# First FFN of a hybrid decoder layer: early weight splits spread over the whole stage, gate and up in turns, and the column tiles of the mixing stage split there too

## The chip, the cores and the metric

The kernel runs on one core of a Trainium2 chip, in one launch. The metric is the device time in microseconds (us), from the median of several executions; a further execution is recorded by the hardware profiler.

## The reference

One layer of a decoder trunk on 1024 tokens of width 1024, with 16 learned meta tokens put in front. It computes, in float32:

```python
h = h + 0.5 * swiglu(rms_norm(h, ffn1_norm), ffn1_w_in, ffn1_w_out)
u = rms_norm(h, mix_norm) @ w_in
hq, hf, hi, hg, sq, sk, sv = split(u)            # 7 groups of 512 columns
o = concat([hgrn2(hq, hf, hi, hg), stick_breaking(sq, sk, sv)])
h = h + o @ w_out
h = h + 0.5 * swiglu(rms_norm(h, ffn2_norm), ffn2_w_in, ffn2_w_out)
```

`swiglu(x) = (silu(x @ W_gate) * (x @ W_up)) @ W_out` with 2816 hidden columns. `hgrn2` is a gated linear recurrence of 4 heads, and `stick_breaking` is a strictly causal attention of 8 heads whose weights are products of sigmoids. The meta tokens are dropped at the end.

## The kernel before, in words

**Precision.** TensorE multiplies in a float32 format of reduced precision. Each operand is therefore split into a high part (a cast on ScalarE, line 357 in the FFNs, 226 for other weights) and a low part (a subtraction on VectorE, lines 359 and 228), and each product is three matmuls: high by high, low by high, high by low. A weight tile comes raw from DRAM, and is split just before it is used.

**First FFN, input side** (`fast_in`). The 1040 positions lie in thirds of 352, 344 and 344 columns. Two thirds are computed together by a scheme of seven products in place of eight: a *quad* is a block of 256 hidden columns of gate or of up. Its seven products are named by the activation operands B11, T2, B21, T3, T1, T4 and B22, and accumulate in three PSUM banks: B11 and B21 in `qa`, T2, T3 and T4 in `qb`, T1 and B22 in `qc`. Between products VectorE copies a partial sum out of a bank (`kept`, line 458: u2 after T2, u3 after T3), and the next product in that bank waits for it. The weights of a quad are four raw blocks `a11, a21, a22, a12` and four sums of them, made by POOL (`made`, line 372). The remaining third (352 columns, *plain*) is multiplied with the raw blocks in the ordinary way, in bank `qd`. For the first three pairs of quads (the *openers*, about 75 to 165 us) the plain part runs ahead, and the pairs run afterwards, gate quad first, then up quad; from about 165 us the eight remaining pairs carry the plain products inside the quad (`also`), so that a quad has eleven products of twelve matmuls.

The order on TensorE is written out by hand (`manual_schedule`). On the other engines the framework's scheduler orders the instructions by its own model of time; `tc.issue_after(ins)` adds that what a block traces on the engine of `ins` is queued behind `ins`.

**Early splits.** `split_ahead` takes blocks of 128 by 512 weights through a small pipeline: load (groups of four blocks, one group ahead), for some blocks a sum on POOL (line 193), cast on ScalarE (168) and subtraction on VectorE (169) into a tile `both` (three buffers), store of both parts to DRAM (163). Each `next` of the generator advances it by one block. The kernel before does this for 28 blocks: the seven weight operands of four quads of the second FFN (`quad_group`), which later loads them split (`parted2`). The steps are advanced by `taken`, called after each eviction of the first FFN's main loop, once more than six quads are done: one step for each eviction until they are used up. `turn_x`, advanced by `between` after each quad, transposes x into a DRAM tensor.

**The middle.** `col_tile` and `split_w` (lines 209 to 229) load and split a weight tile of w_in (128 columns, 512 KB) or w_out (256 KB), or load its two parts where they lie in DRAM already (`self.parted`, empty in the kernel before). They are used by the attention's projections, by `hgrn_fill` (16 tiles of the recurrence: kinds v, f, q, g of four heads), which fills TensorE beside the attention, and by `mix_out`, which multiplies with w_out, half of it beside the recurrence. Two tiles (columns 2560 and 3072) are taken ahead, during step A22 of the first FFN's output side (`early_w`).

Of the kernel before, what the change touches and what calls it, by code (L numbers as in the profile page):

```python
# [20 lines left out]
P = 128  # L21
D = 1024
# [17 lines left out]
class Block:  # L40
# [141 lines left out]
    def quad_group(self, pool, w_in, col, dst):  # L182

        nc = self.nc
        views = [
            w_in[512 * h : 512 * h + 512, col + P * i : col + P * i + P]
            .rearrange("(k p) f -> p k f", p=P) for i, h in ((0, 0), (1, 0), (1, 1), (0, 1))
        ]
        s = {}

        def kept(name, op, x, y):
            t = s[name] = pool.tile([P, 512], F32, tag="sum", name="sum", bufs=3)
# [149 lines left out]
    def fast_in(self, ops, n, w_in, actD, openers, ev0, open_ev, feed=None, plain=None,  # L342
                between=lambda: None, after_opened=lambda: None, taken=lambda at: None):
# [44 lines left out]
        def weights(col, opened, also):  # L388
# [9 lines left out]
            s1 = made(a21, nc.gpsimd.tensor_add, a22)  # L398
            s2 = made(s1, nc.gpsimd.tensor_sub, a11)
            yield operand(s2)  # L400
            yield operand(a12)
            yield operand(made(a11, nc.gpsimd.tensor_sub, a21))
            yield operand(s1)
            yield operand(a22)
            yield operand(made(a12, nc.gpsimd.tensor_sub, s2))
            if also:
                yield operand(a21)
# [24 lines left out]
        def quad(col, take, opened=None, also=None):  # L432
            w = weights(col, opened, also)
# [13 lines left out]
            def first():  # L447
                p = go("a", "B11", True)
                p1 = ev0.tile([P, n], F32, tag="p1", name="p1", bufs=2 if plain else 2 * openers)
# [3 lines left out]
            def kept(name, x, y):  # L453
                if opened == "second":
                    t = wp.tile([P, n], F32, tag="s", name=name, bufs=3)
                else:
                    t = ev["p"].tile([P, n], F32, tag=name, name=name)
# [45 lines left out]
        def pair(f, opened=None, also=(None, None)):  # L503
# [32 lines left out]
            def combined():  # L536
# [20 lines left out]
                quad(f * P, gate, opened, also[0]),  # L557
                quad(D_FF + f * P, up, opened and "second", also[1]),
            ]

        ahead = range(0, 2 * openers, 2)
        if plain:
# [7 lines left out]
            for f in ahead:  # L570
                for q in pair(f):
                    drain(q)
                    between()
        else:
# [10 lines left out]
            for i in range(0, 2 * openers, 2):  # L585
                live = opened[i : i + 2]
                while live:
                    live = [q for q in live if next(q, live) is not live]
# [276 lines left out]

    def hgrn_fill(self, xh, xl, pool, dst):

        nc = self.nc
        plan = [(kind, h) for h in range(4) for kind in "vfqg"]
        first = {"v": 1024, "f": 512, "q": 0, "g": 1536}  # L870
# [23 lines left out]
        def weights(i):  # L894
            return self.col_tile(self.a["w_in"][0], first[plan[i][0]] + P * plan[i][1])
# [439 lines left out]
    def mix_out(self, k0, plan, o, ws, hD, hT, pool):  # L1335
# [4 lines left out]
        def part(m, half, k, kept):  # L1340
            c0, n = HALVES[half]
            if k == 0:
                if m not in ws:
                    ws[m] = self.split_w(
                        self.a["w_out"][0][k0 * P : (k0 + 4) * P, m * P : (m + 1) * P]
                        .rearrange("(k p) f -> p k f", p=P)
# [95 lines left out]
    def run(self):  # L1442
# [21 lines left out]
        with ExitStack() as c0:  # L1464
            with ExitStack() as c1:
                with tc.manual_schedule(engines={nc.tensor.engine}), ExitStack() as c2:
# [17 lines left out]
                    def ahead_of_time(pool):  # L1484

                        groups = []
                        for i in range(2):
# [9 lines left out]
                    def open_ev():  # L1497
# [4 lines left out]
                        turning.append(ahead_of_time(self.pool("ahead", ctx=c2)))  # L1502
                        return ev

                    def taken(at):
                        if len(seen) > 6:
                            with tc.issue_after(at.ins):
                                next(turning[1], None)

                    seen = []  # L1510

                    def between():
                        seen.append(len(seen))
# [29 lines left out]
                with tc.manual_schedule(engines={nc.tensor.engine}), ExitStack() as c2:  # L1543
# [62 lines left out]
                    def between(step, q):  # L1606
# [7 lines left out]
                        elif step == "A22":  # L1614
# [254 lines left out]
```

## Time and profile before

| | us |
|---|---|
| median of 3 runs | 2096.02 |
| lowest and highest | 2088.78, 2096.17 |
| the profiled execution | 2096.82 |
| its span in the trace | 2095.1 |

The stages in the profiled execution, by the trace: first FFN's input side to about 500 us, its output side to about 756, attention projections to about 925, attention with the recurrence's projections to about 1230, recurrence and output projection to about 1450, second FFN to the end. A row of the page or of a group names line, engine, operation, output tile and inputs, shape and count, then busy time and mean duration, then the idle time before the group and what ended it. A row of the timeline gives the start and the duration in us, and in brackets the idle time of the engine before it and what released it. PE is TensorE's matmul, PEld its weight load, DVE VectorE, ACT ScalarE, POOL GpSimd, SP the engine that issues most transfers.

### The profile page before, as it was taken

The page shows a single profiled execution, that of the slowest core. Times are in us where ns is not written, and L with a number is a line of the kernel's source. Part 1 is how long each engine was busy: PE and PEld are TensorE (multiplying, and loading weights), DVE is VectorE, ACT ScalarE, POOL GpSimd, SP SyncE. Part 2 cuts the span into 40 slices and gives each one's busy share as a digit, 9 for nine tenths or more (in the row PEclk, how much of TensorE's full clock was granted, in tenths as well). Part 3 has the DMA queues.
Part 4 walks back from the last instruction along what each step waited for, and adds up shares of the span by engine and source line. Part 5 has one row for each costly group of instructions (what it writes and reads, how often), then busy time and mean ns, then how long its engine had stood idle before and what let it go on. Part 6 is the DMA issues. An engine that isn't in the chain of part 4 may idle for free.

```text
span 2095.1 us, 32297 instructions
## 1 busy us (share of the span) xinstructions
PE 2028.8 (97%) x11520; PEld 1833.9 (88%) x11520; DVE 1397.9 (67%) x2140; ACT 899.7 (43%) x1860; POOL 646.5 (31%) x710
## 2 busy tenths in 40 slices
PE   7899999999999999999999999899999999999998
PEld 7899999999999989997888888778788888888887
DVE  6775874455479962338787857657567676676774
ACT  8543443323455643356666632334123233234443
POOL 2465664453000001234343310101155454440000
PEclk9999999999999999999999999999999999999999
DMA  7543874233866825443545162345633233359464
GB/s 193 172 154 123 276 253 144 89 96 119 296 208 211 258 82 176 135 172 97 145 126 141 62 231 74 96 121 176 210 117 111 93 108 101 106 197 328 137 196 136
DMA packets 280440, 328.39 MB, mean 157 GB/s; under 512 B 25911, under 2 KB 196279, under 8 KB 280279
## 3 DMA queue, kind: packets, MB, share of 16 engines
q1 hardware_dynamic: 262582, 275.88, 42.9%
q0 software_dynamic: 16656, 50.44, 6.5%
q8 instruction: 91, 1.49, 0.3%
q14 instruction: 71, 0.57, 0.1%
q10 hardware_dynamic: 1040, 0.00, 0.0%
HBM read 229.00 MB, written 97.25 MB: 156 GB/s over the span
## 4 chain that ended last, share of the span: by engine, by line
PE 77%; DVE 5%; issue 2%; ACT 1%; DMA 1%; POOL 1%; SPq 0%; DVEq 0%; POOLq 0%; ACTq 0%
PE o L697 16%; PE qb L413 11%; PE qa L413 8%; PE qc L413 7%; PE proj L243 5%; PE proj L244 5%; PE proj L245 5%; PE qd L413 4%; PE o L663 4%; PE flip L1177 2%; PE lvl L946 2%; PE wo L244 1%; PE wo L245 1%; PE wo L243 1%; DVE keep L1323 1%
## 5 line engine op out<-in xcount | busy, mean ns | idle before, releaser
L413 PE MATMUL qb<-T,wh 128*128 128x344 f32 (+1 forms) x1056 | 310.6, 357 | 9.1 <-DVE u L458 7.7
L359 DVE TENSOR_TENSOR wl<-s,wh 128x512 fp32r<-128x512 f32 x160 | 188.4, 1177 | 110.8 <-ACT wh L357 108.6
L413 PEld LDWEIGHTS qb<-T,wh 128*128 128x128 f32 x1056 | 193.2, 189 | 34.4 <-ACT wh L357 8.5
L697 PE MATMUL o<-parts 128*128 128x512 f32 x924 | 209.9, 389 | 0.0
L413 PE MATMUL qa<-B,wh 128*128 128x344 f32 (+1 forms) x696 | 206.2, 359 | 0.0
L243 PE MATMUL proj<-xh,wh 128*128 128x344 f32 (+2 forms) x576 | 204.9, 356 | 0.0
L697 PEld LDWEIGHTS o<-parts 128*128 128x128 f32 x924 | 173.3, 188 | 36.0
L244 PE MATMUL proj<-xh,wl 128*128 128x344 f32 (+2 forms) x576 | 199.4, 346 | 1.1 <-DVE wl L228 1.1
L245 PE MATMUL proj<-xl,wh 128*128 128x344 f32 (+2 forms) x576 | 198.7, 345 | 0.0
L413 PE MATMUL qb<-T,wl 128*128 128x344 f32 (+1 forms) x528 | 188.0, 356 | 0.0
L413 PE MATMUL qd<-X,wh 128*128 128x352 f32 x704 | 182.8, 327 | 1.6 <-DVE X L772 1.6
L359 DVE TENSOR_TENSOR wl<-raw,wh 128x512 fp32r<-128x512 f32 x160 | 148.5, 932 | 53.8 <-ACT wh L357 51.3
L357 ACT CAST wh<-s 128x512 fp32r<-128x512 f32 x160 | 99.4, 622 | 181.2 <-PE qb L413 130.0
L357 ACT CAST wh<-raw 128x512 fp32r<-128x512 f32 x160 | 98.6, 619 | 173.1 <-PE qc L413 88.5
L697 PE MATMUL o<-t,w 128*128 128x344 f32 x924 | 150.1, 323 | 3.8 <-DVE t L627 2.1
L697 PEld LDWEIGHTS o<-t,w 128*128 128x128 f32 x924 | 147.3, 189 | 5.5 <-DVE t L627 3.1
L413 PEld LDWEIGHTS qa<-B,wh 128*128 128x128 f32 x696 | 126.5, 188 | 15.5
L1323 DVE TENSOR_TENSOR_SCAN keep<-keep 128x144 f32<-128x144 f32 (+6 forms) x112 | 128.6, 1151 | 6.5 <-ACT keep L1319 4.4
L372 POOL TENSOR_TENSOR s<-raw 128x512 f32<-128x512 f32 x80 | 113.5, 1418 | 60.9 <-DVE wl L359 48.8
L1328 POOL TENSOR_TENSOR sig<-sig,keep 128x144 f32<-128x144 f32 (+3 forms) x64 | 87.0, 1360 | 138.8 <-DVE keep L1323 85.9
L413 PEld LDWEIGHTS qd<-X,wh 128*128 128x128 f32 x704 | 126.7, 192 | 1.8 <-DVE X L772 1.8
L413 PE MATMUL qa<-B,wl 128*128 128x344 f32 (+1 forms) x348 | 124.1, 357 | 0.7 <-DVE wl L359 0.7
(342 smaller groups left out, 4601.3 us busy)
## 6 DMA issues: line engine op xcount, KB each, us to landing
raw<-in_ffn_w_in_dram SPq DMA_DIRECT2D x184, 256.0 KB, 3.2
raw<-in_ffn_w_out_dram SPq DMA_DIRECT2D x176, 256.0 KB, 3.9
w2in<-both SPq DMA_DIRECT2D x28, 512.0 KB, 3.8
raw<-in_w_in_dram SPq DMA_DIRECT2D x28, 512.0 KB, 4.2
ks<-kD SPq DMA_DIRECT2D x32, 260.0 KB, 5.7
wh<-w2in SPq DMA_DIRECT2D x27, 256.0 KB, 3.1
wl<-w2in SPq DMA_DIRECT2D x27, 256.0 KB, 3.2
ak<-in_ffn_w_out_dram SPq DMA_DIRECT2D x22, 256.0 KB, 5.3
```

The lines of the kernel that those rows point to most:

```text
L243: nc.tensor.matmul(ps, wh[:, s], xs, start=k == 0, stop=False)
L244: nc.tensor.matmul(ps, wl[:, s], xs, start=False, stop=False)
L245: nc.tensor.matmul(ps, wh[:, s], xl[:, k, c0 : c0 + n], start=False, stop=k == nk - 1)
L357: nc.scalar.copy(hi, src)
L359: nc.vector.tensor_sub(lo, src, hi.bitcast(F32))
L372: op(t, x, y)
L413: nc.tensor.matmul(ps, a[:, k, :], b[:, k0 + k, :], start=start and k == 0 and i == 0, stop=k == 3 and i == 2, skip_group_check=True,)
L663: nc.tensor.matmul(ps[m], y[:, s], z, start=f == 0 and e == 0, stop=f == D_FF // P - 1 and e == 2,)
L697: nc.tensor.matmul(banks[bank][m], y[:, m * P : (m + 1) * P], z, start=start and q == 0 and e == 0, stop=q == nq - 1 and e == 2, skip_grou ...
L946: nc.tensor.matmul(ps[:, j, :], KB[:, META + c * P : META + (c + 1) * P], QA[:, c * P : (c + 1) * P], start=True, stop=True,)
L1323: nc.vector.tensor_tensor_scan(out=kv, data0=kv, data1=kv, initial=1.0 if last else keep[:, end : end + 1], op0=ALU.mult, op1=ALU.bypass,)
L1328: nc.gpsimd.tensor_mul(sig, sig, keep[:, 1 : nk + 1])
```

## The change

- The early splits are 78 blocks: 34 halves of 17 tiles of w_in (columns 2560, 3072 and 2048, and all of the recurrence's but the first two) and 16 tiles of w_out come first, then the 28 blocks of before.
- `taken` counts the evictions from the start. The first 36 advance nothing (12 of the plain openers, 24 of the opener pairs); from there 81 steps are spread over 88 evictions. POOL's sums of the first FFN are marked too, and each step is queued behind the latest marked instruction of every engine.
- The opener pairs run gate and up in turns, one product of each. Up's sums, its first partial sum and the partial sums u2, u3 get buffers of their own.
- In the main loop the second plain product with block a22 comes before T4 rather than after it.
- `quad_group` makes its last sum earlier, with two buffers for sums rather than three.
- The two tiles in step A22 are taken at its second and fourth rounds, rather than its sixth and eighth, and are not queued behind an eviction.

```diff
         return views, [
             ...
             (dst[2], lambda r: kept(2, sub, s[1], r[0])),
+            (dst[6], lambda r: kept(4, sub, r[3], s[2])),
             (dst[5], lambda r: r[2]),
             (dst[3], lambda r: kept(3, sub, r[0], r[1])),
-            (dst[6], lambda r: kept(4, sub, r[3], s[2])),
         ]
...
-        def made(x, op, y):
-            t = wp.tile([P, 4, P], F32, tag="s", name="s", bufs=3)
-            op(t, x, y)
+        def made(x, op, y, turns):
+            if turns == 2:
+                t = self.ahead.tile([P, 4, P], F32, tag="raw", name="s", bufs=8)
+            else:
+                t = wp.tile([P, 4, P], F32, tag="s", name="s", bufs=3)
+            taken(op(t, x, y), False)
             return t
...
+                if turns:
+                    yield
                 u2 = kept("u2", p1, go("b", "T2", True))
+                if turns:
+                    yield
                 take(0, 0, go("a", "B21", False), None)
+                if turns:
+                    yield
...
             take(1, 1, go("c", "T1", True), u3)
             yield
+            if also:
+                ready.append(next(w))
+                d = alone(None, ready[0], 1, True)
             take(1, 0, go("b", "T4", False), p1)
             yield
-            if also:
-                d = alone(None, last[0], 1, True)
             take(0, 1, go("c", "B22", False), u2)
...
+        def in_turns(live):
+            while live:
+                live = [q for q in live if next(q, live) is not live]
...
             for f in ahead:
-                for q in pair(f):
-                    drain(q)
-                    between()
+                in_turns(pair(f, None, (None, None), True))
+                between()
+                between()
...
+                        for col in [2560, 3072, 2048] + self.columns_of_heads()[2:]:
+                            t = self.parted[col] = self.dram.tile([P, 2, D], F32, name=f"win{col}")
+                            for h in range(2):
+                                pieces.append((
+                                    t[:, :, 512 * h : 512 * h + 512],
+                                    w_in[512 * h : 512 * h + 512, col : col + P]
+                                    .rearrange("(k p) f -> p k f", p=P),
+                                ))
+                        for k0 in (4, 0):
+                            for m in range(KT):
+                                ...
+                                self.parted[k0, m] = t
+                        groups += self.plain_groups(pieces)
...
-                    def taken(at):
-                        if len(seen) > 6:
-                            with tc.issue_after(at.ins):
+                    def taken(at, step=True):
+                        marks[at.ins.engine] = at.ins
+                        if not step:
+                            return
+                        seen.append(at)
+                        i = len(seen) - first
+                        if i > 0 and steps_ahead * i // hooks > steps_ahead * (i - 1) // hooks:
+                            with ExitStack() as c4:
+                                for ins in marks.values():
+                                    c4.enter_context(tc.issue_after(ins))
                                 next(turning[1], None)
+                    first, hooks, steps_ahead = 12 + 24, 88, 81
...
-                            if q in (5, 7):
-                                col = {5: 2560, 7: 3072}[q]
-                                with tc.issue_after(self.evicted.ins):
-                                    early_w.append(self.col_tile(a["w_in"][0], col))
+                            if q in (1, 3):
+                                early_w.append(
+                                    self.col_tile(a["w_in"][0], {1: 2560, 3: 3072}[q])
+                                )
```

More of the change, by code (lines that the diff above doesn't have):

```diff
@@ L386, in parted, with weights @@
             return got
-        def weights(col, opened, also):
+        def weights(col, opened, also, turns):
             if opened:
@@ L430, in plain_quad, with quad @@
                 take(i, ps)
-        def quad(col, take, opened=None, also=None):
-            w = weights(col, opened, also)
+        def quad(col, take, opened=None, also=None, turns=False):
+            w = weights(col, opened, also, turns)
             ps, ready, last = {}, [], []
@@ L448, in first @@
                 p = go("a", "B11", True)
-                p1 = ev0.tile([P, n], F32, tag="p1", name="p1", bufs=2 if plain else 2 * openers)
+                if turns == 2:
+                    p1 = ev["p"].tile([P, n], F32, tag="p1", name="p1")
+                else:
+                    p1 = ev0.tile(
+                        [P, n], F32, tag="p1", name="p1", bufs=2 if plain else 2 * openers
+                    )
                 self.last_p1 = nc.scalar.copy(p1, p)
@@ L501, in plain_pair, with pair @@
             return gate, up
[L503 removed]
+        def pair(f, opened=None, also=(None, None), turns=False):
             sg = {}
@@ L556, in pair @@
             return [
-                quad(f * P, gate, opened, also[0]),
-                quad(D_FF + f * P, up, opened and "second", also[1]),
-            ]
+                quad(f * P, gate, opened, also[0], turns and 1),
+                quad(D_FF + f * P, up, opened and "second", also[1], turns and 2),
+            ]
+        def in_turns(live):
+            while live:
+                live = [q for q in live if next(q, live) is not live]
         ahead = range(0, 2 * openers, 2)
@@ L585, in fast_in @@
             for i in range(0, 2 * openers, 2):
-                live = opened[i : i + 2]
-                while live:
-                    live = [q for q in live if next(q, live) is not live]
+                in_turns(opened[i : i + 2])
             after_opened()
```

38 lines of the change are left out of this document (25 added, 13 removed).

## The prediction

> **What bounds the kernel now.** I read the page first, then the stretches of the span (busy time of each engine, granted clock, DMA share), then, where TensorE lost time, the groups and the timeline. The page:
>
> ```profile
> PE 2028.8 (97%) x11520; PEld 1833.9 (88%) x11520; DVE 1397.9 (67%) x2140; ACT 899.7 (43%) x1860; POOL 646.5 (31%) x710
> ```
>
> TensorE (PE) is busy 97% of the span, so an edit that adds no matmul can only win back the time in which PE waits, or runs slowly. The next rows are stretches: length, busy time (and instructions) of PE, PEld, DVE, ACT and POOL, granted clock, DMA share and GB/s. The last three are narrow.
>
> ```profile
> 75.00:100.00 25.00, 20.41 (x109) 19.11 (x108) 11.54 (x18) 9.57 (x19) 12.24 (x10) 0.86 0.85 246
> 205.00:306.00 101.00, 96.28 (x600) 95.16 (x599) 83.06 (x101) 43.72 (x81) 65.62 (x64) 0.98 0.74 255
> 306.00:500.00 194.00, 194.00 (x1231) 193.43 (x1230) 98.79 (x145) 65.42 (x122) 94.88 (x102) 1.00 0.34 109
> 735.00:756.00 21.00, 17.71 (x104) 16.90 (x103) 18.69 (x41) 10.56 (x27) 0.00 (x0) 0.93 0.20 63
> 87.30:94.20 6.90, 6.45 (x20) 5.75 (x21) 4.71 (x6) 3.96 (x8) 6.18 (x5) 0.51 0.80 233
> 251.20:254.60 3.40, 3.40 (x14) 3.40 (x13) 3.37 (x5) 0.62 (x1) 2.71 (x3) 0.50 0.75 258
> 753.00:756.40 3.40, 3.40 (x14) 3.40 (x13) 1.07 (x3) 0.46 (x1) 0.20 (x1) 0.50 0.02 5
> ```
>
> From 306 to 500 us (first FFN, no early splits) PE never waits: 1231 matmuls in 194 us, 0.158 us each, so a product of twelve takes 1.9 us. A quad of the main loop is eleven products (seven, and four for the plain columns), 132 matmuls or 20.8 us; from 205 to 306 us, 600 matmuls, lie about 4.5 quads, and all but a few of the 28 early splits. The last three rows are spells at half clock, each behind a long PE wait; they cost about half their length: 3.3, 1.7 and 1.7 us.
>
> **Edit 1: splits bound behind the work before them, gate and up in turns (75 to 165 us).** The old early splits were ordered on one engine only, so some floated forward:
>
> ```profile
> 86.49 0.62 ACT L168 CAST both<-early 128x512 fp32r<-128x512 f32 x1 [7.32 <-DMA early<-in_ffn_w_in_dram]
> ...
> 87.68 0.66 PE L413 MATMUL qc<-T,wh 128*128 128x344 f32 x1 [3.82 <-ACT wh L357]
> ```
>
> ACT stood 7.32 us with an early cast at the head of its queue, until that cast's load landed; the cast that PE needed stood behind it, and PE waited 3.82 us. The new `marks` queue every step behind the latest marked instruction of ACT, DVE and POOL, and the first step comes after 36 evictions, behind all openers. So the wait and its half-clock spell go: 3.8 + 3.3 = 7.1 us. Two more openers lose time differently:
>
> ```profile
> L413 PE MATMUL qb<-T,wh 128*128 128x344 f32 x110 | 28.4, 322 | 3.0 <-DVE u L458 3.0
> ```
>
> T4 accumulates into the bank that DVE must first read as u3, and only T1 (1.9 us) lies between. In turns the up quad puts two products more there, 5.7 us in all: the 3.0 us go. What turns may add: up's first product comes second instead of eighth, so its four blocks are wanted earlier.
>
> ```profile
> 74.74 2.92 SPq L364 DMA_DIRECT2D raw<-in_ffn_w_in_dram  x5
> ```
>
> These five loads go out from 74.74 us, while the first quad's product starts at about 75. The cost lies between 0 (up's blocks are now requested before gate's sums, so they move forward in SP's queue) and 3.8 us (a wait as long as the one removed). The order of requests speaks for the low end: I take 1.5. Sum of edit 1: 7.1 + 3.0 − 1.5 = 8.6 us gained.
>
> **Edit 2: 78 blocks on 88 hooks, and the second plain product put ahead of T4 (165 to 500 us).** The dense stretch now loses this:
>
> ```profile
> L413 PE MATMUL qb<-T,wh 128*128 128x344 f32 x100 | 26.7, 331 | 4.7 <-DVE u L458 4.7
> ```
>
> The same wait of T4, 4.7 us in 4.5 quads, and behind the longest of them the spell at 251.2 us: 6.4 us together. The longest, with DVE's queue before it:
>
> ```profile
> 247.80 1.88 DVE L359 TENSOR_TENSOR wl<-raw,wh 128x512 fp32r<-128x512 f32 x1
> 249.61 0.50 DVE L458 TENSOR_TENSOR u<-qb,p 128x344 f32<-128x344 f32 x1
> ...
> 250.26 0.40 PE L413 MATMUL qb<-T,wh 128*128 128x344 f32 x1 [2.10 <-DVE u L458]
> ```
>
> The new order puts a plain product (1.9 us) between T1 and T4. It hides less than that, though: the plain product uses the same weights as T4, and their low half is the subtraction directly ahead of u3 in DVE's queue (ends 249.68, u3 ends 250.11). The wait moves to the plain product and is only 0.43 us shorter. So 4.7 − 4.5 × 0.43 = 2.8 us stay in 4.5 quads, 0.6 per quad.
>
> How long does such lag last now? Twelve hooks fall in two quads, so 88 hooks are 14.7 quads, and 81 steps are 5.5 a quad; the old rate was 28 in 4.5, 6.2. The bytes per time hardly change: 78 stores of 512 KB and 66 loads of 256 KB in 306 us are 190 GB/s, against 28 and 16 in 101 us, 187 GB/s, at a share of 0.74; more DMA waits are not due. VectorE's price:
>
> ```profile
> L359 DVE TENSOR_TENSOR wl<-raw,wh 128x512 fp32r<-128x512 f32 x18 | 19.6, 1090 | 1.5 <-ACT wh L357 1.5
> ...
> L169 DVE TENSOR_TENSOR both<-sum,both 128x512 fp32r<-128x512 f32 x16 | 18.6, 1163 | 3.0 <-ACT both L168 2.8
> L169 DVE TENSOR_TENSOR both<-early,both 128x512 fp32r<-128x512 f32 x12 | 12.6, 1048 | 3.3 <-ACT both L168 3.3
> ```
> ```profile
> L359 DVE TENSOR_TENSOR wl<-raw,wh 128x512 fp32r<-128x512 f32 x32 | 23.4, 733 | 32.9 <-ACT wh L357 31.5
> ```
>
> The same subtraction takes 1090 ns in the dense stretch and 733 after it. The 50 new blocks come first and need no POOL sums (the old 28 need 16), so their price lies between 0.73 and 1.16 us; I take 0.9, nearer the row without sums. DVE is then busy 51% (98.79 of 194) plus 5.0 of 20.8 us, some 75%, for 50 of 78 blocks (9.4 quads), and 82% as in the dense stretch for the last 28 (5.3 quads). Lag: 5.3 × 0.6 = 3.2 us, and 9.4 × 0.2 = 1.9 (0.2 is a choice between 0 at 51% and 0.6 at 82%). 6.4 − 5.1 = 1.3 us gained. Bounds: 6.4 gained if nothing waits, and the old price on all 14.7 quads (6.4 / 4.5 = 1.42 a quad, 20.9 us), 14.5 lost. Two-slot sums and the reordered T4 operand only bind POOL, which was busy 65% at most: nothing, or one sum late (1.3 us) at worst. ACT's 50 more casts of 0.62 us lift it from 34% to about 50%: hidden.
>
> **Edit 3: what leaves the middle.** At the end of the first FFN two column tiles were split in VectorE's busiest stretch (18.69 of 21 us); the first:
>
> ```profile
> 736.19 1.23 DVE L228 TENSOR_TENSOR wl<-raw,wh 128x1024 fp32r<-128x1024 f32 x1
> ...
> 747.86 2.00 PE L697 MATMUL o<-t,w 128*128 128x344 f32 x11 [1.58 <-DVE t L627]
> ...
> 751.58 0.42 PE L697 MATMUL o<-t,w 128*128 128x344 f32 x1 [1.71 <-DVE w L627]
> ```
>
> Twice 1.23 us leave a queue that is 3.3 us late, and the spell at 753 us (1.7) should go with the wait: 4.1, I take 4.0 (0 to 5.0). Four loads of 512 KB replace two on SP's queue, earlier, at a DMA share of 0.20. Further waits on splits:
>
> ```profile
> L244 PE MATMUL proj<-xh,wl 128*128 128x512 f32 x16 | 6.5, 404 | 1.1 <-DVE wl L228 1.1
> ```
> ```profile
> L244 PE MATMUL wo<-oH,wl 128*128 128x512 f32 x3 | 1.8, 584 | 1.5 <-DVE wl L228 1.5
> ```
>
> 2.6 us, near 781 and 1396 us. The split operands now come by DMA and need free buffers before they start; a raw tile of 512 KB took 4.2 us to land:
>
> ```profile
> raw<-in_w_in_dram SPq DMA_DIRECT2D x28, 512.0 KB, 4.2
> ```
>
> So each could also lose 2 us if its memory comes free as late as the old cast. I take 1.7 gained (−4 to 2.6). Between 925 and 1230 us the waits are these, and two of them follow a tile's split:
>
> ```profile
> L1177 PE MATMUL flip<-ident,sig 128*128 128x128 f32 x288 | 47.9, 275 | 11.2 <-DVE wu L1292 8.6 <-DVE wm L1292 2.5
> ```
> ```profile
> L228 DVE TENSOR_TENSOR wl<-raw,wh 128x1024 fp32r<-128x1024 f32 x14 | 20.8, 1485 | 10.1 <-ACT wh L226 10.0
> ```
> ```profile
> 1096.13 1.23 DVE L228 TENSOR_TENSOR wl<-raw,wh 128x1024 fp32r<-128x1024 f32 x1 [0.79 <-ACT wh L226]
> ...
> 1101.71 0.41 PE L1177 MATMUL flip<-ident,sig 128*128 128x128 f32 x2 [1.45 <-DVE wu L1292]
> ...
> 1163.72 1.23 DVE L228 TENSOR_TENSOR wl<-raw,wh 128x1024 fp32r<-128x1024 f32 x1 [0.19 <-ACT wh L226]
> ...
> 1168.66 0.52 PE L1177 MATMUL flip<-ident,sig 128*128 128x128 f32 x3 [1.83 <-DVE wu L1292]
> ```
>
> 20.8 us leave VectorE; I count the two waits, 3.2 us (0, if the scans alone make them, to 6, half of 11.2). The eight output tiles beside the recurrence I put at 0 (−2 to 2, the size of the two waits above): PE there follows a chain of short steps, not the splits.
>
> **Sum.** 8.6 + 1.3 + 4.0 + 1.7 + 3.2 = 18.8 us. The profiled execution took 2096.8 us (span 2095.1, 1.7 around it), 0.8 above the median: 2096.8 − 18.8 = **2078.0 us**.
>
> **Rivals.** *The old price on every hook*: each of 14.7 quads loses 1.42 us as now. For it: the wait's cause, the subtraction ahead of u3, stays. Against: 50 blocks without sums, and none of the quads near 180 us waits now. Edit 2 then loses 14.5: 2078.0 + 1.3 + 14.5 = 2093.8 us, no measurable change. *Slower: lag that drops the clock, quad after quad.* At 250.26 a wait of 2.10 us was followed by half clock: 2.1 + 1.7 = 3.8 us. If VectorE at 75 to 82% lags that far in every quad, the stage loses 14.7 × 3.8 = 55.9 instead of 6.4, so 2078.0 + 1.3 + 49.5 = 2128.8 us; it decides from about ten quads on (38 − 6.4 − 17.5, 14 slower). For it: the wait that shows it. Against: one spell in 4.5 quads, at a higher rate. The Trainium skill (TensorE: Matmul & The Clock Gate, HAM oscillation — how this bites in real kernels) warns of idle gaps above about 3.4 us only; by that rule a gap of 2.1 us keeps the clock and this rival would cost 2.1 × 14.7 = 30.9, 2103.8 us. The trace disagrees: 2.10 us sufficed. *The middle gives nothing*, since the loaded operands come as late as the old splits: 4.0 + 1.7 + 3.2 − 4.0 = 4.9 is lost of the sum (the emptied queue at 735 us stays): 2082.9 us.
>
> **How the numbers follow.** About 0.5%, 10.5 us, is what a measurement of this kernel can tell from no change. Chances: the forecast and its neighbours down to −10.5 us 0.53, the empty middle 0.11, the old price 0.23, the clock rival 0.13. Faster 0.64, same 0.23, slower 0.13. Low end: all good bounds, 10.1 + 6.4 + 5.0 + 2.6 + 6 + 2 = 32.1, 2065 us. High end: the old price with the turns' cost at 3.8, 2096 us. The clock rival is left out.
>
> **What would show it.** Right: no ACT wait on an early load and clock 1.00 from 85 to 95 us; no wait for u in the openers; early splits from about 170 to 475 us at an even rate; no L226 or L228 on the tiles of the recurrence; clock 1.00 from 735 to 760 us; flip's waits under 9 us. Wrong: PE waits above 1 us in most quads from 170 to 475 us with half-clock spells, PE waiting on a loaded wh or wl, or SP's queue standing before wh while other loads queue.

## The result and the profile after

| | before | after |
|---|---|---|
| median, us (5 runs each) | 2096.17 (2088.78 to 2098.8) | 2104.59 (2102.44 to 2108.25) |
| ratio of times | | 1.0042, 95% interval 1.0025 to 1.0058 |
| profiled execution, us | 2096.82 | 2104.59 |
| its span | 2095.1 | 2102.9 |

The change costs 8.4 us, 0.42%, where a gain of 18.8 us was forecast. That is less than the 10.5 us that the prediction named as the least a measurement can tell, but the interval lies clear of 1. The next table cuts the two spans at the first matmul of each stage, so that its rows sum to the spans.

| stage | before | after | gained | forecast |
|---|---|---|---|---|
| start (ahead of the openers' seven products) | 75.16 | 76.45 | −1.29 | 0 |
| openers | 95.86 | 94.96 | +0.90 | +8.6 |
| main loop of the first FFN | 345.63 | 360.79 | −15.16 | +1.3 |
| output side, first part | 84.88 | 84.88 | 0 | 0 |
| output side, second part, with step A22 | 155.60 | 155.97 | −0.37 | +4.0 |
| projections | 180.95 | 179.61 | +1.34 | +1.7 (both waits) |
| attention with the recurrence's projections | 303.96 | 299.63 | +4.33 | +3.2 |
| recurrence and output projection | 202.22 | 199.20 | +3.02 | (above) |
| second FFN | 650.86 | 651.35 | −0.49 | 0 |

The start lies between 74.7 and 78.4 us in the kernels run here, and its 1.3 us are within that. The page of after shows TensorE as well filled as before. The loss is many small waits, and 5.0 us more busy time for the same 11520 matmuls:

```profile
PE 2033.8 (97%) x11520; PEld 1836.0 (87%) x11520; DVE 1423.4 (68%) x2157; ACT 900.8 (43%) x1877; POOL 644.9 (31%) x710
```

The stretches of after, columns as in the prediction:

```profile
75.00:100.00 25.00, 19.40 (x103) 17.94 (x102) 12.67 (x17) 6.31 (x12) 11.34 (x11) 0.86 0.53 148
205.00:306.00 101.00, 96.67 (x607) 94.76 (x606) 73.95 (x100) 44.62 (x83) 46.41 (x51) 1.00 0.94 300
306.00:500.00 194.00, 185.36 (x1152) 182.08 (x1151) 150.01 (x178) 82.72 (x154) 119.55 (x118) 0.99 0.76 257
```

From 306 to 500 us PE was never idle before; now it does 1152 matmuls where it did 1231. The DMA share from 205 to 306 us is 0.94 against 0.74.

**Main loop.** First two groups of the stretch from 205 to 306 us of before, ScalarE's early casts, and then the same cast in the main loop of after (165 to 500 us), with the groups in which PE waits:

```profile
L168 ACT CAST both<-sum 128x512 fp32r<-128x512 f32 x15 | 9.2, 615 | 11.0 <-DMA w2in<-both 10.9
L168 ACT CAST both<-early 128x512 fp32r<-128x512 f32 x10 | 6.2, 615 | 6.3 <-DMA w2in<-both 6.3
```
```profile
L416 PE MATMUL qd<-X,wh 128*128 128x352 f32 x464 | 122.4, 327 | 3.4 <-ACT xts L849 3.4
L416 PE MATMUL qd<-X,wl 128*128 128x352 f32 x232 | 75.8, 327 | 7.1 <-DVE wl L359 7.1
L359 DVE TENSOR_TENSOR wl<-raw,wh 128x512 fp32r<-128x512 f32 x58 | 67.2, 1158 | 9.5 <-ACT wh L357 9.0 <-DMA raw<-in_ffn_w_in_dram 0.3
L168 ACT CAST both<-early 128x512 fp32r<-128x512 f32 x62 | 38.1, 615 | 65.5 <-DMA win<-both 27.3 <-DMA wout<-both 19.4 <-DVE both L169 6.0
```

A cast needs a free `both` tile, and a tile is free when its store to DRAM has landed. ScalarE stands 65.5 us with the cast at the head of its queue, 46.7 us of them for stores. The row was there before (10.9 and 6.3 us for w2in's stores), and I read past it. From 205 to 306 us alone, with 25 casts in both kernels, the stores account for 17.2 us before and 25.3 after. What stands behind the cast is late, here the copy of transposed x (L849):

```profile
256.38 0.62 ACT L168 CAST both<-early 128x512 fp32r<-128x512 f32 x1 [1.91 <-DMA win<-both]
...
260.50 0.57 ACT L849 COPY xts<-xt 128x512 f32<-128x512 f32 x1
...
261.12 0.43 PE L416 MATMUL qd<-X,wh 128*128 128x352 f32 x1 [0.80 <-ACT xts L849]
```

The transfers issued from 205 to 306 us, with count, size and median time to landing, before and then after:

```profile
w2in<-both SPq DMA_DIRECT2D x27, 512.0 KB, 3.7
early<-in_ffn_w_in_dram SPq DMA_DIRECT2D x7, 256.0 KB, 4.3
```
```profile
win<-both SPq DMA_DIRECT2D x25, 512.0 KB, 5.1
early<-in_w_in_dram SPq DMA_DIRECT2D x21, 256.0 KB, 5.3
early<-in_w_out_dram SPq DMA_DIRECT2D x5, 256.0 KB, 5.5
```

27 stores and 7 loads were 16.0 MB; 25 stores and 26 loads are 19.9 MB, 197 GB/s instead of 158.

**Openers.** SP's queue, PE's and POOL's in after, and a stretch of 11 us:

```profile
76.10 2.94 SPq L364 DMA_DIRECT2D raw<-in_ffn_w_in_dram  x5
```
```profile
87.00 0.66 PE L416 MATMUL qb<-T,wh 128*128 128x344 f32 x1 [2.43 <-ACT wh L357]
89.35 0.66 PE L416 MATMUL qb<-T,wl 128*128 128x344 f32 x1 [1.70 <-DVE wl L359]
```
```profile
67.71 5.13 POOL L375 TENSOR_TENSOR s<-raw 128x512 f32<-128x512 f32 x1 [5.25 <-DMA raw<-in_ffn_w_in_dram]
...
74.51 1.56 POOL L375 TENSOR_TENSOR s<-raw 128x512 f32<-128x512 f32 x1
83.24 1.28 POOL L375 TENSOR_TENSOR s<-raw 128x512 f32<-128x512 f32 x1 [7.17 <-DMA raw<-in_ffn_w_in_dram]
```
```profile
84.00:95.00 11.00, 6.88 (x29) 6.22 (x28) 5.15 (x6) 2.62 (x5) 5.87 (x7) 0.69 0.47 133
```

The cast held by an early load is gone, and so is every wait for u3 in this stage, but the blocks of the first pair land later than they are wanted. SP issues five loads at 76.10 us, when POOL's third sum has ended (74.51 + 1.56 = 76.07), and 0.35 us ahead of the pair's first product at 76.45. In the kernel before they left 0.42 us ahead (74.74 against 75.16), so the new order did not move them forward. POOL's first sum took 5.13 us here and 5.10 before, where the median of the kernel's 80 sums of two raw blocks is 1.30. POOL then waits 7.17 us for one of the loads, the sum is late, its cast and subtraction are late, and PE waits twice. A granted clock of 0.69 from 84 to 95 us shows a spell at half clock again, as behind the wait of before.

**Step A22.** The stage of after runs some 16 us later (its output side starts at 532.2 us, not 516.7), so the stretch that answers to 739 to 752 us there is about 723 to 736 us of before. SP's queue, the activation's landing and the stretch, before:

```profile
723.37 0.39 SPq L219 DMA_DIRECT2D raw<-in_w_in_dram  x1
724.85 0.32 SPq L617 DMA_DIRECT2D act<-act15T  x1
...
725.93 0.42 SPq L219 DMA_DIRECT2D raw<-in_w_in_dram  x1
```
```profile
act<-act15T SPq DMA_DIRECT2D x1, 172.0 KB, 3.5
```
```profile
720.00:741.00 21.00, 21.00 (x139) 21.00 (x138) 17.91 (x39) 15.97 (x35) 2.14 (x4) 1.00 0.84 260
```

And after, with the row of PE's wait:

```profile
739.98 0.38 SPq L214 DMA_DIRECT2D wh<-win  x1
...
741.36 0.43 SPq L214 DMA_DIRECT2D wl<-win  x1
...
743.15 0.67 SPq L634 DMA_DIRECT2D act<-act15T  x1
```
```profile
act<-act15T SPq DMA_DIRECT2D x1, 172.0 KB, 9.7
```
```profile
739.00:752.00 13.00, 13.00 (x85) 13.00 (x84) 10.16 (x21) 8.24 (x19) 2.13 (x4) 1.00 0.94 314
```
```profile
758.92 1.40 PE L279 MATMUL spread<-diag,ones_d 128*128 128x128 f32 x6 [3.17 <-DVE diag L276]
```

The engines were 84% busy there already. Nothing keeps the four loads of after apart (two lie between the rows shown), so SP sends 2 MB in a row where before sent 0.5 MB twice; the activation behind them takes 9.7 us to land instead of 3.5, and further on PE waits 3.17 us for the norm.

**The middle** did what was forecast. The attention's stretch, after:

```profile
L1199 PE MATMUL flip<-ident,sig 128*128 128x128 f32 x288 | 47.8, 275 | 7.5 <-DVE wu L1314 4.9 <-DVE wm L1314 2.5
L228 DVE TENSOR_TENSOR wl<-raw,wh 128x1024 fp32r<-128x1024 f32 x1 | 1.2, 1212 | 0.0
```

One split is left of 14, and flip waits 7.5 us instead of 11.2.

### The profile page after: what moved, and what is told of

It reads as the page before. It is cut to its first block, busy times and chain, and to the rows that moved or that the text cites. A ratio compares the mean times of both kernels' runs of the same rounds, so it can differ in the third digit from the quotient of the medians.

```text
span 2102.9 us, 32545 instructions
## 1 busy us (share of the span) xinstructions
PE 2033.8 (97%) x11520; PEld 1836.0 (87%) x11520; DVE 1423.4 (68%) x2157; ACT 900.8 (43%) x1877; POOL 644.9 (31%) x710
## 4 chain that ended last, share of the span: by engine, by line
PE 67%; DVE 4%; issue 1%; DMA 1%; ACT 1%; POOL 1%; SPq 0%; DVEq 0%; POOLq 0%
PE o L714 16%; PE qb L416 8%; PE qa L416 6%; PE qc L416 6%; PE proj L243 5%; PE proj L244 5%; PE proj L245 5%; PE o L680 4%; PE lvl L968 2%; PE flip L1199 2%; PE wo L243 1%; PE wo L244 1%; PE wo L245 1%; DVE keep L1345 1%; PE oacc L1269 1%
## 5 line engine op out<-in xcount | busy, mean ns | idle before, releaser
L359 DVE TENSOR_TENSOR wl<-s,wh 128x512 fp32r<-128x512 f32 x160 | 192.3, 1202 | 100.6 <-ACT wh L357 98.6
L245 PE MATMUL proj<-xl,wh 128*128 128x344 f32 (+2 forms) x576 | 198.7, 345 | 0.0
L359 DVE TENSOR_TENSOR wl<-raw,wh 128x512 fp32r<-128x512 f32 x160 | 160.1, 1005 | 19.0 <-ACT wh L357 17.5
L416 PE MATMUL qd<-X,wl 128*128 128x352 f32 x352 | 116.1, 330 | 10.7 <-DVE wl L359 10.6
```

What stands on the lines that cost most here:

```text
L245: nc.tensor.matmul(ps, wh[:, s], xl[:, k, c0 : c0 + n], start=False, stop=k == nk - 1)
L359: nc.vector.tensor_sub(lo, src, hi.bitcast(F32))
L416: nc.tensor.matmul(ps, a[:, k, :], b[:, k0 + k, :], start=start and k == 0 and i == 0, stop=k == 3 and i == 2, skip_group_check=True,)
```

## The experiments

My theory after the result had three parts: the stores of 50 more blocks fill the DMA engines and hold ScalarE (main loop); turns ask for up's blocks before they can be there (openers); the loads in step A22 crowd out others. The rivals were the splits' own work on VectorE and POOL, and the new place of the plain product. Stage lengths decide, since the total of single executions of the kernel before moved between 2088.8 and 2099.7 us; where no ratio is given, the total is that of one execution.

**1. The fifty blocks split, but not stored.** The 50 new blocks are loaded and split, their store is left out, and the mixing stage splits its tiles itself as before.

```diff
-            if split:
+            if split and split[0] is not None:
                 nc.sync.dma_start(split[0], split[1].bitcast(F32))
...
-                        groups += self.plain_groups(pieces)
+                        self.parted.clear()
+                        groups += self.plain_groups([(None, v) for _, v in pieces])
```

> The changed kernel, in which the 50 new blocks are loaded, cast and subtracted at the same hooks but never stored; the middle splits its tiles itself again. The main loop of the first FFN (first plain product behind the openers to the first product of the output side) takes 345.6 us before and 360.8 us after. Theory (transfers: stores of 512 KB each fill the DMA engines to 0.93-0.95, come late, and hold the three buffers for which ScalarE's queue waits 63.7 us): the loop falls to 349-353 us, what is left being the last 28 blocks; no wait for the transpose copies on ScalarE. Rival (VectorE and ScalarE work: 50 more casts and subtractions): the loop stays at 357-361 us, since all that work is still there.

```profile
205.00:306.00 101.00, 101.00 (x645) 100.90 (x645) 69.70 (x103) 46.00 (x84) 53.55 (x60) 1.00 0.62 185
306.00:500.00 194.00, 187.48 (x1167) 184.53 (x1166) 148.25 (x185) 85.48 (x159) 114.39 (x109) 0.99 0.60 200
```

Main loop 348.7 us, just under the theory's range; total 2101.68. With the stores gone PE is never idle from 205 to 306 us, although all the casts and subtractions are there. Leaving out the stores wins back 12.1 us. From 306 to 500 us PE still waits, so that is another cause.

**2. Only the 28 blocks of before, on the new hooks.**

```diff
-                        groups += self.plain_groups(pieces)
+                        self.parted.clear()
...
-                    first, hooks, steps_ahead = 12 + 24, 88, 81
+                    first, hooks, steps_ahead = 12 + 24, 88, 31
```

> The changed kernel with the 28 blocks of before alone, spread over the same 88 evictions (31 steps), and the middle splits its tiles itself. Theory (transfers): main loop 346-349 us, below e1 by the little that casts and subtractions cost. Rival (engine work): 346-349 us as well, but then e1 lies 8 us or more above it. If the plain product ahead of T4 is what costs, both e1 and e2 stay well above 350.

```profile
205.00:306.00 101.00, 100.77 (x642) 100.38 (x641) 67.85 (x85) 38.35 (x71) 60.03 (x64) 1.00 0.56 182
306.00:500.00 194.00, 192.75 (x1222) 191.89 (x1221) 130.65 (x171) 74.68 (x141) 102.98 (x105) 1.00 0.48 158
```

Main loop 341.2 us, 4.4 better than before and better than I expected; total 2092.96, ratio 0.9994 (0.998 to 1.0009). So spreading the splits and the new place of the plain product, together, are good. The medians do not show it (0.2 us apart). The two tiles of step A22, split there at its second and fourth round, make that part 157.6 us long (155.6 before), which takes up 2.0 us; the executions of this kernel spread from 2083.96 to 2096.31 us. Step by step from the kernel before, the main loop goes −4.4 for these two, +7.5 for loading and splitting 50 more blocks (run 1 against this one), +12.1 for storing them: 15.2 lost. The three add up because each is the difference to the step before.

**3. The changed kernel with the plain product behind T4 again.**

```diff
-            if also:
-                ready.append(next(w))
-                d = alone(None, ready[0], 1, True)
             take(1, 0, go("b", "T4", False), p1)
             yield
+            if also:
+                d = alone(None, last[0], 1, True)
```

> The changed kernel with the plain product on block a22 behind T4 again, as before. Theory (transfers, and late weight halves in the last third): the place of this product matters little; the waits of the plain product for the low half of its weights come back as waits of T4 for u3, one subtraction later: main loop 361-366 us. Rival (the new place makes the plain product wait): main loop 352-357 us.

A group of the main loop:

```profile
L416 PE MATMUL qb<-T,wh 128*128 128x344 f32 x360 | 93.9, 325 | 10.0 <-DVE u L466 7.9 <-ACT both L168 2.1
```

Main loop 357.2 us, just above the rival's range and well under the theory's; total 2092.28, 12.3 us under the changed kernel's, 3.6 of them from the main loop and the rest from other stages (openers 92.9, step A22's part 152.1). The wait for u3 is back at 7.9 us, and the waits of `qd` for wl (7.1 us in after) are gone. Under this DMA load the new order is 1.9 to 3.6 us worse, by one trace of the old order against three of the new (359.1 us in run 4, 359.6 in run 6, 360.8 in after); whether it is better without that load was not tried by itself.

**4. The changed kernel with the opener pairs one after the other.**

```diff
             for f in ahead:
-                in_turns(pair(f, None, (None, None), True))
-                between()
-                between()
+                for q in pair(f):
+                    drain(q)
+                    between()
```

> The changed kernel with the opener pairs one quad after the other again, everything else kept. The opener stage (first product of the openers to the first plain product behind them) takes 95.9 us before and 95.0 after. Theory (turns cost up's late blocks what binding the early casts saves): without turns the wait of 3.8 us and its half-clock spell are gone and only the two waits for u3 (3.0 us) stay: 88-90 us. Rival (the first pair waits for its blocks in either order, because they are requested late): 94-96 us.

POOL's first sum, SP's five loads ahead of the openers, and a narrow stretch:

```profile
65.29 1.39 POOL L375 TENSOR_TENSOR s<-raw 128x512 f32<-128x512 f32 x1 [4.63 <-DMA raw<-in_ffn_w_in_dram]
```
```profile
69.91 4.26 SPq L364 DMA_DIRECT2D raw<-in_ffn_w_in_dram  x5
```
```profile
87.30:94.20 6.90, 6.90 (x47) 6.88 (x46) 3.54 (x7) 3.53 (x8) 1.01 (x2) 1.00 0.94 259
```

Openers 87.5 us, total 2093.61. The bound early splits gain 8.4 us (95.9 to 87.5), and full clock holds from 87.3 to 94.2 us where before had 0.51. The turns lose 7.4 us net, though they save the 3.0 us of u3 that are back here; in runs 1, 2, 3 and 6, which have turns at every pair too, the openers take 92.9 to 94.1 us, so the net loss lies between 5.4 and 7.4.

The order of the products is not all that differs, though. The five loads go out at 69.91 us here, 6.5 us ahead of the first product (76.42) instead of 0.35: POOL's first sum took 1.39 us and not 5.13, and began 2.4 us earlier against that product. In all five traces with turns at the first pair that sum took 4.9 to 5.6 us and the loads left under 0.5 us ahead. The long sum alone does not cost the openers: in run 5, without turns, it took 4.14 us, the loads left 2.9 us ahead, and the openers still took 87.5 us; in the kernel before the loads were as late as in after, and PE waited for none of up's blocks. So the loss comes when late loads meet an order that wants up's blocks early. Whether turns would cost anything with the loads 6.5 us ahead, no run shows. Nor was it tried what decides the length of that sum: in the five traces in which it took 1.4 us, the operation of VectorE that began just behind it took 1.6 us instead of 0.5.

**5. As 4, with five `both` tiles instead of three.**

```diff
-                both = pool.tile([P, 2, 512], F32R, tag="both", name="both", bufs=3)
+                both = pool.tile([P, 2, 512], F32R, tag="both", name="both", bufs=5)
```

> The kernel without turns (opener stage 87.5 us, main loop 359.1 us), with five buffers for the split blocks rather than three. If ScalarE's queue, which stands 62 us behind stores that have not landed, is the way by which the transfers reach TensorE: the wait for stores falls under 15 us and the main loop to 348-353 us. If the transfers are simply too many (share 0.94, everything late): the wait moves to the loads, main loop 356-361 us.

```profile
205.00:306.00 101.00, 100.36 (x637) 99.72 (x636) 76.36 (x97) 44.83 (x83) 54.91 (x59) 1.00 0.96 312
306.00:500.00 194.00, 184.24 (x1142) 180.72 (x1141) 149.94 (x183) 84.26 (x160) 111.74 (x108) 0.99 0.75 254
```
```profile
L168 ACT CAST both<-early 128x512 fp32r<-128x512 f32 x62 | 38.1, 618 | 32.4 <-DMA win<-both 15.1 <-DMA wout<-both 9.3 <-DVE u L543 4.8
```

Main loop 353.7 us against 359.1 in run 4, total 2085.37. The DMA share is as high as ever, 0.96, but PE hardly waits in the first stretch: what hurt there was ScalarE's queue held by a cast without a buffer, not the full engines as such. Neither expectation was met in full: the row still has 24.4 us of waiting for stores, and the loop lies just above the theory's range. The buffers win back 5.4 us, under half of what leaving out the stores did (12.1); the stretch from 306 us loses as before, and how the stores act there was not separated.

**6. The changed kernel, its column stores 4 KB in a piece instead of 2.**

```diff
...
-                            t = self.parted[col] = self.dram.tile([P, 2, D], F32, name=f"win{col}")
+                            t = self.parted[col] = self.dram.tile([P, 2, 2, 512], F32, name=f"win{col}")
...
-                                    t[:, :, 512 * h : 512 * h + 512],
+                                    t[:, h],
```

> The changed kernel with the 34 column blocks laid out so that a store writes 4 KB in one piece for each partition rather than two pieces of 2 KB. If the pieces make these stores slow (5.1 us to land against 4.2 of the others): they land in under 4.5 us, the DMA share from 205 to 305 us falls from 0.94 to under 0.85 and the main loop from 360.8 to 351-356 us. If the bytes alone count: share 0.92-0.95 and 358-362 us.

```profile
205.00:306.00 101.00, 97.32 (x612) 95.42 (x611) 75.00 (x99) 44.16 (x82) 48.92 (x54) 1.00 0.94 304
```
```profile
win<-both SPq DMA_DIRECT2D x34, 512.0 KB, 5.3
```

Main loop 359.6 us, total 2100.32, share and landing time as in the changed kernel (0.94; 5.1 us). The rival holds: bytes count here, not the length of the pieces.

**7. As 4, with 50 blocks in all:** none of the recurrence's 14 tiles (28 halves), only columns 2560, 3072 and 2048 beside w_out and the 28 of before, and 53 steps.

```diff
-                        for col in [2560, 3072, 2048] + self.columns_of_heads()[2:]:
+                        for col in [2560, 3072, 2048]:
...
-                    first, hooks, steps_ahead = 12 + 24, 88, 81
+                    first, hooks, steps_ahead = 12 + 24, 88, 53
```

> Without turns, and with 50 early blocks: the three column tiles used first, the 16 tiles of w_out and the 28 of the second FFN, 53 steps over 88 evictions; the recurrence's tiles are split in the middle again. Theory (transfers): bytes per time fall to two thirds, share near 0.7, main loop 342-347 us; opener stage 87-88; attention stage back at 304; recurrence and output projection 197-199 us: 2076-2082 us in all. Rival (the waits come with any early block): main loop above 350 us, 2086 us or more.

```profile
205.00:306.00 101.00, 101.00 (x645) 100.89 (x644) 64.10 (x92) 41.62 (x78) 53.85 (x59) 1.00 0.76 244
```

Main loop 342.0 us, total 2080.94 us, ratio 0.994 (0.9919 to 0.996). The 22 other new blocks keep most of their worth in the middle (projections 179.6, recurrence and output 198.7), and cost the main loop 0.8 us (342.0 against 341.2 in run 2). The attention goes back to 304.3: 28 column halves cost 17 us in the main loop (359.1 against 342.0) and gained 4.6 there.

**8. As 7, with turns for the second and third opener pair only.** The edit to the openers, against the changed kernel:

```diff
             for f in ahead:
+                if f == 0:
+                    for q in pair(f):
+                        drain(q)
+                        between()
+                else:
-                in_turns(pair(f, None, (None, None), True))
+                    in_turns(pair(f, None, (None, None), True))
...
```

> Fifty blocks as in the run before, but only the first opener pair runs gate and up one after the other; the second and third pair run in turns, one product of each. Theory: turns cost time only at the first pair, where up's blocks are asked for before they can have landed; at the later pairs the requests are ahead, so nothing is late, and the two waits of T4 for the partial sum u3 (1.69 and 1.68 us, at 115 and 144 us) go. Openers 84.0 to 85.5 us instead of 87.5, total 2076 to 2080 us. Rival: up's blocks come late at every pair, openers 88 to 92 us, total 2081 to 2086 us. The main loop stays at 342 +- 1.5 us either way.

Openers 84.3 us as the theory has it, both waits for u3 gone; total 2081.51 us, ratio 0.993 (0.9909 to 0.995), above the 2076 to 2080 expected, since PE waited 2.66 us in step A22 (part 156.1 against 153.4 in run 7). Two executions were under 2080 us and two above 2083. So the turns' price is all the first pair's: they gain 3.2 us at the two others (87.5 to 84.3; run 10 repeats it) and lose 10.6 at the first (94.96 to 84.34; 8.6 to 9.8 by runs 1, 2, 3 and 6), there together with loads that leave late (run 4).

**9. As 7, with five `both` tiles.** The edit is that of run 5.

> Fifty blocks with openers one after the other, and five buffers for the split parts instead of three. Theory: at a DMA share of about 0.76 the stores land in time for three buffers, so the main loop stays at 342 +- 1.5 us and the total at 2078 to 2083 us. Rival: ScalarE still stands before full buffers here, and the one wait of 2.00 us at 348 us and some smaller ones come from it: main loop 337.5 to 340 us, total 2076 to 2079 us.

Main loop 341.2 us, total 2084.06 us, ratio 0.9946 (0.9931 to 0.9961), a little above the range given. At this rate of stores a further buffer brings nothing that can be told.

**10. As 8, with the second tile of step A22 taken at its ninth round instead of its fourth** (the expectation counts rounds from 0).

```diff
-                            if q in (1, 3):
+                            if q in (1, 8):
...
-                                    self.col_tile(a["w_in"][0], {1: 2560, 3: 3072}[q])
+                                    self.col_tile(a["w_in"][0], {1: 2560, 8: 3072}[q])
```

> The fifty blocks and openers of the run with late turns; only the second of the two split tiles of step A22 is taken at its eighth round instead of its third, so that SP issues four loads of 512 KB in two pairs with other loads between, instead of all four in a row. The order on the other engines does not change. Theory: the four loads in a row hold the DMA engines, and the activation and weight tiles behind them come late, which delays the norm for which PE waits (2.66 us in the run before, 3.17 us in the changed kernel). Apart, that wait falls below 1.5 us and the stage from the middle of the output side to the first projection takes 152.5 to 154.5 us instead of 156.1; total 2077 to 2080 us. Rival: the wait comes from VectorE's or ScalarE's own queue, and stays at 2 to 3 us, stage 155.5 to 156.5 us, total 2080 to 2083 us.

The activation's landing (issued to about 730 us) in run 8, then in this one:

```profile
act<-act15T SPq DMA_DIRECT2D x1, 172.0 KB, 11.6
```
```profile
act<-act15T SPq DMA_DIRECT2D x1, 172.0 KB, 6.5
```

Only the order of SP's queue differs. The wait for the norm is gone, a wait of 1.43 us for another activation stays, and the part takes 151.65 us instead of 156.1. With the loads in a row the part was not always as bad: 152.1 to 153.4 us in runs 3, 4, 5, 7 and 9, 155.2 to 156.1 in the changed kernel and runs 6 and 8. In all eight traces with the loads in a row the activation takes 7.3 to 11.6 us to land, and PE waits 0.3 to 3.2 us for the norm; in the kernel before and run 1, without such a row, it takes 3.5 and 4.5 us there, and PE does not wait for the norm. So the row of loads opens the way to the wait; what sets its length was not taken apart (landings of 9.7 us go with waits of 1.06 and 3.17). This run is one trace of the cure. Total 2078.55 us (2073.29 to 2080.69), ratio 0.9922 (0.9906 to 0.9938), below both kernels; its interval and run 8's overlap, so the totals do not show the cure.

## Why the prediction was wrong

The 2104.6 us lie above the whole range of 2065 to 2096 us. Of the 26.5 us between the forecast gain and the measured spans, 16.5 are Edit 2's, 7.7 Edit 1's, 4.4 step A22's and 1.8 of the start and the second FFN; the middle gave 3.8 more than forecast.

**Edit 2 failed, and decided it.** The step was "The bytes per time hardly change … more DMA waits are not due". It spread 66 loads over 306 us and set against them 16 loads in 101 us, but nine of those 16 had gone out before that stretch. What went out in the 101 us was 158 GB/s of early splits, and it became 197; the share rose from 0.74 to 0.94, stores landed in 5.1 us instead of 3.7, and with three buffers ScalarE stood. That three buffers were already short was in the trace of before (17.2 us of ScalarE waiting for w2in's stores), and the prediction priced the 50 casts only by their 0.62 us of work: "hidden". The loss of 15.2 us nearly equals the rival *the old price on every hook* (14.5), but that is luck: that rival had T4's wait for u3 in every quad, and this wait is gone from after. What it said of lag on VectorE fits the smaller part, the 7.5 us of loading and splitting without stores (run 1 against 2), in which PE waits 5.3 us for `qd`'s wl. The blocks' own subtraction was sized right, 0.9 us taken and 0.93 measured; the quads' subtraction with raw input, 0.73 us where nothing was beside it, now takes 1.16 over the whole stage (the row of L359 above), and from 384 us on PE's waits for a22's low half are the longest of the loop:

```profile
L169 DVE TENSOR_TENSOR both<-early,both 128x512 fp32r<-128x512 f32 x62 | 57.5, 928 | 18.8 <-ACT both L168 18.3 <-DMA raw<-in_ffn_w_in_dram 0.3 <-DMA w2in<-both 0.2
```
```profile
386.83 0.46 PE L416 MATMUL qd<-X,wl 128*128 128x352 f32 x1 [2.29 <-DVE wl L359]
```

That the wait moves from T4 to the plain product was right, and under load it costs as much there. With the 28 blocks alone (run 2) almost none of it is left, 4.4 us gained where 1.3 were forecast for all 78.

**Edit 1 was right in one half.** Bound splits: forecast 7.1, measured 8.4. The turns' cost was bounded by 3.8 and taken at 1.5; measured, they lost 8.6 to 10.6 us at the first pair. The step that failed is "up's blocks are now requested before gate's sums, so they move forward in SP's queue": the loads left 0.35 us ahead of the pair's first product in after and 0.42 in the kernel before, in both when POOL's third sum had ended, so they did not move forward. They left earlier (6.5 us ahead in run 4, 2.9 in run 5) where POOL's first sum was shorter; the prediction did not ask what releases them. Two waits, several small ones and a half-clock spell followed, and the bound had been one wait long.

**Edit 3** was right where VectorE's time was the reason (attention +4.3, recurrence and output +3.0, projections +1.3: 8.7 against 4.9; runs 1 and 2, which split in the middle again, have the lengths of before). At step A22 the split's removal worked, but "Four loads of 512 KB replace two on SP's queue, earlier, at a DMA share of 0.20" read the share from the wrong stretch: 0.20 is that of 735 to 756 us, and the loads go out ahead of it, where it was 0.84 (720 to 741 us). The wait came back as 3.17 us for the norm. In run 10, with the loads apart, the part is 3.95 us shorter than before, about the 4.0 forecast.

**The clock rival** did not come: the main loop of after has two half-clock spells, not one in most quads. A wait and the 7 us around or behind it, first in after, then in run 7:

```profile
502.16 0.43 PE L416 MATMUL qd<-X,wl 128*128 128x352 f32 x1 [1.81 <-DVE wl L359]
```
```profile
500.00:507.00 7.00, 5.19 (x24) 4.90 (x23) 5.64 (x7) 1.62 (x3) 2.24 (x2) 0.76 0.45 184
```
```profile
732.86 0.90 PE L279 MATMUL spread<-diag,ones_d 128*128 128x128 f32 x6 [2.26 <-DVE diag L276]
```
```profile
731.00:738.00 7.00, 5.14 (x34) 5.14 (x35) 6.96 (x20) 4.86 (x14) 0.00 (x0) 1.00 0.15 52
```

Behind a wait of 1.81 us the granted clock was 0.76, and behind one of 2.26 us it stayed at 1.00; it also stayed at 1.00 in run 4 behind the same wait of 1.81 us at the same place (494.55 us). So the length alone does not settle it in this range. The Trainium skill (TensorE: Matmul & The Clock Gate, HAM oscillation — how this bites in real kernels) gives the rule as no idle gaps above about 3.4 us; of the waits shown only the 3.82 us of the openers in the kernel before reach that, and still there were spells at half clock behind shorter ones, so a shorter wait has to be counted with the risk of one.

## What to carry to other kernels

Before work is added to a stage for its idle engines, list what a buffer's reuse waits for: an in-order engine that holds an instruction for a store's landing delays everything behind it, and the row for it is often already in the profile, small. Compare DMA load by what is issued in one and the same stretch, the one in which the new transfers will stand, not by stage means, and keep bulk loads apart in the queue: here four in a row went with a small transfer behind them that landed late. Before an order is changed, ask what releases the loads that it needs; here it was one sum, whose length changed from trace to trace. And try the parts of a bundled change one by one: here the spread and bound splits, the turns of the later pairs and 22 of the 50 new blocks gain, and the bundle was slower only by what was added to them.

## What the runs showed that was not expected

Landing time grew with the load: a store of 512 KB took 3.7 us at a share of 0.74 and 5.1 us at 0.94. At 0.96, with two more buffers, PE hardly waited from 205 to 306 us all the same (run 5). Doubling the store's piece from 2 to 4 KB changed neither share nor time (run 6). One sum on POOL took 1.4 us in five traces and 4.1 to 5.6 in the seven others, and the loads behind it left between 0.35 and 6.6 us ahead of the openers' first product.
